# A third buffer for the A and D blocks of the first MLP product, and their loads moved up

## The chip, the cores and the metric

The kernel runs on one core of one Trainium2 chip. The metric is the device time of one execution in microseconds (us). The engines are named as the profile names them: PE is TensorE (PEld its weight loads), DVE is VectorE, ACT is ScalarE, POOL is GpSimd and SP is SyncE. SP and POOL do no arithmetic here that matters; they issue transfers.

## What is computed

One decoder layer over 512 positions of width 1024 in float32: RMSNorm, an input projection whose columns feed a gated linear recurrence (HGRN2) and a block-sparse attention (MoBA), an output projection, cross-attention into 256 memory tokens, and an MLP with a squared ReLU, each with its residual. The change lies in the MLP:

```python
h = rms_norm(x, norm_mlp[l])
x = x + jnp.square(jax.nn.relu(h @ w_ff1[l])) @ w_ff2[l]
return rms_norm(x, norm_final)
```

`w_ff1` is 1024 x 4096 and `w_ff2` is 4096 x 1024.

## The kernel before

**Split weights.** Each 128 x 1024 unit of weights is loaded in float32 into a raw buffer (`wr`, or `wA`, `wB`, `wC`, `wc`, `wD`, `wd` in the first MLP product) and split into a high part that ACT writes (`wh`) and a low part that DVE writes (`wl = raw - wh`). Each product is then three matmuls: high by high, high by low, low by high.

**The first MLP product** (`f1_group`, line 1107) runs in eight groups j. In each, a 2 x 2 block product is made with seven products instead of eight, the way of Strassen and Winograd, on sums and differences of blocks. A group is seven steps of 24 matmuls. Of the weights it needs seven operands, in this order of splitting: A, B, D, C, A, c, D. `f1_load` (277) loads a block by a transfer on SP; for B and c a second transfer on POOL adds another block into the buffer when the first has landed (`accum_op`, 283). The second A is the sum B + C and the second D is D + A; DVE makes both in place, in the buffers of A and D (`f1_add`, 285). So the buffers of A and D are read until late in a group: that of A until the split of the fifth operand, that of D until that of the seventh.

**Buffers.** `raw_tile` (227) gives them out in turn: B, C and c have the three buffers of tag `raw`, A and D the two of tag `rawl` in the pool `late`, which takes the place of the pool `early` once that is closed (1034). A load waits until the last reader of its buffer is done.

**The order** around the change is written out by hand. `need` (315) runs at the start of step s of the program with u the unit that TensorE takes next, and prepares the unit two ahead (`SPLIT_AHEAD`): `f1_prep` (288) issues its split and, by s, loads for the next group. Instructions of one engine run in the order of the program, and SP's and POOL's transfers are issued in the order of their queues. DVE's queue holds, beside the low parts and the sums, the additions that take the finished products out of TensorE's banks (`evac`); `t <- t, X` is one of them. `more_sums` (222) issues further transfers that nothing in this product reads: sums of blocks of `w_ff2`, written to the tensors `u` (copies on SP, adds on POOL).

**The second MLP product** takes its units in order through `load_unit` (232), from both tags of buffers, two of five from `rawl`.

Of the kernel before, what the change touches and what calls it, by code (L numbers as in the profile page):

```python
# [8 lines left out]
F32 = mybir.dt.float32  # L9
# [6 lines left out]
P = 128  # L16
D = 1024
T = 512
M = 256
# [12 lines left out]
MLP = 8 + 8 + 4 + 8 + 4 + 4 + 4 + 4 + 8 + 8 + 8  # L32
FF2 = MLP + 7 * 8
# [89 lines left out]
def hybrid_layer(ctx: ExitStack, tc: tile.TileContext, xT, memT, ws, vecs, consts, rots, out):  # L123
    nc = tc.nc
    pace = Pace()
    V, A, PE = (pace.engine(e, t) for e, t in ((nc.vector, "dve"), (nc.scalar, "act"), (nc.tensor, "pe")))
    SY, PO = pace.engine(nc.sync, "dma"), pace.engine(nc.gpsimd, "pool")
    cpool = ctx.enter_context(tc.tile_pool(name="cpool", bufs=1))
# [4 lines left out]
    ep = early.enter_context(tc.tile_pool(name="early", bufs=1, reuse_waits="tile"))  # L133
# [36 lines left out]
    raws, his, los, late, n8 = {}, {}, {}, [], [1]  # L170
    state = {"load": 0, "split": 0}
    LOAD_AHEAD, SPLIT_AHEAD, RAWS = 6, 2, 3
# [13 lines left out]
    def two(ap):  # L186
        return ap.rearrange("p (n c) -> p n c", n=2)
# [34 lines left out]
    def more_sums():  # L222
        dma = next(transfers, None)
        if dma is not None:
            tc.add_manual_dep(dma.ins, marks[-2].ins.name, AFTER)

    def raw_tile(name, in_late):
        if in_late:
            return late[0].tile([P, D], F32, tag="rawl", name=name, bufs=2)
        return wpool.tile([P, D], F32, tag="raw", name=name, bufs=RAWS)  # L230

    def load_unit(parts=((0, D),)):
        u = state["load"]
        raws[u] = raw_tile(f"wr{u}", u >= FF2 and (u - FF2) % 5 in (1, 3))
        for a, b in parts:
            SY.dma_start(raws[u][:, a:b], sources[u][:, a:b])
        state["load"] += 1
        if SUMS_FROM <= u < MLP:
            more_sums()
# [6 lines left out]
    def split_raw(u, raw, a, b, eng=None):  # L246
        A.activation(his[u][:, a:b], raw[:, a:b], AF.Copy)

        def lower(hi=his[u], lo=los[u]):
            (eng or V).tensor_sub(lo[:, a:b], raw[:, a:b], hi[:, a:b].bitcast(F32))  # L250
        later(lower)
# [4 lines left out]
    def split_begin():  # L256
        u = state["split"]
        his[u] = wpool.tile([P, D], F32R, tag="whi", name=f"wh{u}", bufs=WBUFS)
        if u < MLP - 4 and u % 4 == 0:
            los[u] = ep.tile([P, D], F32R, tag="wloe", name=f"wl{u}", bufs=1)  # L260
        else:
            los[u] = wpool.tile([P, D], F32R, tag="wlo", name=f"wl{u}", bufs=WBUFS - 1)
        state["split"] += 1
        return u

    def split_unit(eng=None):
        u = split_begin()
        split_part(u, 0, D, eng)
        del raws[u]
# [7 lines left out]
    def f1_load(j, what):  # L277

        r, c = {"A": (0, 0), "B": (0, 0), "C": (1, 1), "D": (1, 0)}[what.upper()]
        t = f1raw[what, j] = raw_tile(f"w{what}{j}", what in "AD")  # L280
        nc.sync.dma_start(two(t), E[r][c][j].rearrange("n p c -> p n c"))
        if what in "Bc":
            nc.gpsimd.dma_start(two(t), E[0][1][j].rearrange("n p c -> p n c"), accum_op=ALU.add)

    def f1_add(j, out, x, y):
        V.tensor_add(f1raw[out, j], f1raw[x, j], f1raw[y, j])

    def f1_prep(j, s):

        split_raw(split_begin(), f1raw[("ABCAcDd" if j == 7 else "ABDCAcD")[s], j], 0, D)  # L290
        if s == 1:
            f1_add(j, "A", "B", "C")
        if j == 7:
            if s == 1:
                f1_load(j, "d")
                state["load"] = FF2
            elif s > 2:
                load_unit()
            if s == 3:
                f1_add(j, "d", "d", "A")  # L300
        elif s == 1:
            f1_load(j + 1, "B")
        elif s == 3:
            f1_add(j, "D", "D", "A")
            f1_load(j + 1, "C")
        elif s == 4:
            f1_load(j + 1, "A")
        elif s == 5:
            f1_load(j + 1, "c")
        elif s == 6:  # L310
            f1_load(j + 1, "D")
        if s in (2, 6):
            more_sums()

    def need(u):
        marks.append(last_mm[0])
        if MLP <= u + SPLIT_AHEAD < FF2:
            f1_prep(*divmod(u + SPLIT_AHEAD - MLP, 7))
            return
        last = MLP if u < MLP else UNITS  # L320
        most = RAWS if u < MLP else RAWS + 2
        want_load, want_split = min(last, u + LOAD_AHEAD + 1), min(last, u + SPLIT_AHEAD + 1)
        while state["split"] < want_split or state["load"] < want_load:
            if state["load"] < want_load and state["load"] - state["split"] < most:
                load_unit()
            elif state["split"] < want_split:
                split_unit()
            else:
                break
        if MLP - 6 <= u < MLP - 2:  # L330
            for what in ("A", "B", "CD", "c")[u - MLP + 6]:
                f1_load(0, what)
# [68 lines left out]
    def fm_stage(u0, act, n, evac, name, groups, order=tuple(range(KT)), o=slice(None)):  # L401


        u = 0
        for size, late in groups:
            accs = []
            early, rest = order[:KT - late], order[KT - late:]
            for j in range(size):
                need(u0 + u + j)
                accs.append(acc_bank(f"{name}{u + j}"))  # L410
                for k in early:
                    fm_k(u0 + u + j, accs[j][:, :n], act, k, k == order[0], k == order[-1], o)
                if not late:
                    evac(u + j, accs[j])
            if late:
                for j in range(size):
                    for k in rest:
                        fm_k(u0 + u + j, accs[j][:, :n], act, k, False, k == order[-1], o)
                    evac(u + j, accs[j])
            u += size  # L420

    def tm_stage(u0, act, ntok, evac, name):

        accs = [acc_bank(f"{name}{t}") for t in range(ntok)]
        for j in range(4):
            need(u0 + j)
            hi, lo = his[u0 + j], los[u0 + j]
            for t in range(ntok):
                for kk in range(2):
                    a_hi, a_lo = act(2 * j + kk)  # L430
                    a_hi, a_lo = a_hi[:, t * P:(t + 1) * P], a_lo[:, t * P:(t + 1) * P]
                    w_hi, w_lo = hi[:, kk * T:(kk + 1) * T], lo[:, kk * T:(kk + 1) * T]
                    st = j == 0 and kk == 0
                    mm(accs[t], a_hi, w_hi, st, False)
                    mm(accs[t], a_hi, w_lo, False, False)
                    mm(accs[t], a_lo, w_hi, False, j == 3 and kk == 1)
                if j == 3:
                    evac(t, accs[t])
# [24 lines left out]
    A.dma_start(vec, vecs)  # L463
    load_x(0)
    load_unit(((0, 2 * P),))
    load_unit(((0, D // 2),))
    load_x(1)
# [138 lines left out]
    lower_bounds()  # L606
    ordered.__exit__(None, None, None)
    need(3)
    for k in range(KT):
        fm_k(3, accs[3], x_act, k, k == 0, k == KT - 1)  # L610
# [3 lines left out]
    u = 4  # L614
# [242 lines left out]
        yield from norm_rows(S, M, rbm, rcm)  # L857

    mem = {}
    rbm = cpool.tile([P, M], F32, name="rbm")  # L860
    rcm = cpool.tile([P, 2], F32, name="rcm")
    fm_stage(u, x_act, T, ev_g, "hg", ONE * 4)
    u += 4
# [523 lines left out]
```

## Time and profile before

| | |
|---|---|
| three timed runs | 758.73, 760.6, 762.17 us; median 760.6 us |
| the profiled execution | 756.95 us, of which its span from first to last instruction is 755.2 us |
| granted TensorE clock, mean | 0.996 of full |
| busy share of the span | PE 97%, PEld 88%, DVE 72%, ACT 55%, POOL 7% |
| transfers | 137.03 MB, mean 181 GB/s |

The rows below come from the profiled execution. A busy share is an average over stages with different limits, so the stage of the change is read by itself, from the load of one group's B to that of the next. An engine that is idle and not waited for costs nothing. Matmuls are pipelined; a row of one lasts about 0.28 us, and the next starts 0.12 us behind it.

### The profile page before, as it was taken

What the parts mean: (1) busy time and instruction counts of PE and PEld (TensorE: products, weight loads), DVE (VectorE), ACT (ScalarE), POOL (GpSimd) and SP (SyncE); (2) the same over time, 40 slices, a digit from 0 to 9 for tenths busy, and PEclk for the clock granted to TensorE, in tenths of its full rate; (3) what the DMA queues carried; (4) which work ended last, traced back from release to release, by engine and by line L of the source; (5) the groups of instructions that cost most, each with busy time, mean ns of one, the idle gap of its engine ahead of it and who ended that gap; (6) DMA issues with size and microseconds to landing.
All of it is one profiled execution on the core that took longest, in us unless ns stands there. A gap on an engine that the chain in (4) does not pass through costs nothing.

```text
span 755.2 us, 11996 instructions
## 1 busy us (share of the span) xinstructions
PE 735.1 (97%) x4696; PEld 664.0 (88%) x4696; DVE 545.5 (72%) x891; ACT 415.5 (55%) x634; POOL 49.4 (7%) x62
## 2 busy tenths in 40 slices
PE   7999999999999999999999999998999999999995
PEld 5888888777787998888888999998899999999995
DVE  6898554887766656767377878786778778877783
ACT  6773447345855454545365655465446655546562
POOL 1000000000111200011000111221110000000000
PEclk9999999999999999999999999999999999999999
DMA  7425334544689996479726688898975655545641
GB/s 274 149 76 167 112 116 135 167 135 132 183 207 238 207 313 258 118 160 278 254 77 147 169 249 221 187 208 215 212 213 169 204 189 193 173 162 168 207 156 57
DMA packets 44441, 137.03 MB, mean 181 GB/s; under 512 B 4544, under 2 KB 6976, under 8 KB 43744
## 3 DMA queue, kind: packets, MB, share of 16 engines
q1 hardware_dynamic: 34944, 110.64, 42.8%
q0 software_dynamic: 8960, 25.17, 19.1%
q8 instruction: 37, 0.61, 0.3%
q10 hardware_dynamic: 480, 0.45, 0.2%
q14 instruction: 20, 0.16, 0.1%
HBM read 134.15 MB, written 35.65 MB: 225 GB/s over the span
## 4 chain that ended last, share of the span: by engine, by line
PE 87%; DMA 4%; ACT 3%; DVE 3%; issue 2%; SPq 0%; DVEq 0%; ACTq 0%
PE X L115 19%; PE Y L115 12%; PE xo L115 7%; PE mkq L115 6%; PE xq L115 6%; PE wo L115 5%; DMA wA<-in_ws_dram 3%; PE hf L115 3%; PE Z L115 3%; PE hg L115 3%; PE mv L115 3%; PE memv L115 3%; PE hq L115 3%; PE hi L115 3%; PE memk L115 2%
## 5 line engine op out<-in xcount | busy, mean ns | idle before, releaser
L115 ACT ACTIVATE wh<-wr 128x1024 fp32r<-128x1024 f32 (+2 forms) x126 | 130.4, 1041 | 121.2 <-PE wo L115 19.6
L115 DVE TENSOR_TENSOR wl<-wr,wh 128x1024 fp32r<-128x1024 f32 (+2 forms) x126 | 151.5, 1205 | 40.7 <-ACT wh L115 26.4
L115 PE MATMUL X<-op,wh 128*128 128x256 f32 x512 | 92.7, 283 | 0.0
L115 PEld LDWEIGHTS X<-op,wh 128*128 128x128 f32 x512 | 79.9, 192 | 0.1
L115 PE MATMUL X<-op,wl 128*128 128x256 f32 x256 | 72.7, 284 | 0.6 <-DVE wl L115 0.6
L200 POOL DMA_DIRECT2D u<-in_ws_dram x32 | 31.0, 968 | 328.5 <-PE hg L115 201.1
L115 PEld LDWEIGHTS X<-op,wl 128*128 128x128 f32 x256 | 49.1, 192 | 0.8 <-DVE wl L115 0.8
L115 PE MATMUL Y<-OS,wh 128*128 128x256 f32 x256 | 47.2, 284 | 0.2 <-ACT t L115 0.2
L115 PE MATMUL X<-OS,wh 128*128 128x256 f32 x256 | 46.5, 283 | 0.0
L115 PE MATMUL Y<-op,wh 128*128 128x256 f32 x256 | 46.2, 283 | 0.0
L115 PEld LDWEIGHTS Y<-OS,wh 128*128 128x128 f32 x256 | 39.9, 192 | 0.5 <-ACT t L115 0.4
L115 PEld LDWEIGHTS Y<-op,wh 128*128 128x128 f32 x256 | 39.9, 192 | 0.0
L115 PEld LDWEIGHTS X<-OS,wh 128*128 128x128 f32 x256 | 39.9, 192 | 0.0
L115 PE MATMUL Y<-op,wl 128*128 128x256 f32 x128 | 36.2, 283 | 0.0
L115 PE MATMUL X<-OS,wl 128*128 128x256 f32 x128 | 36.2, 283 | 0.0
L115 PE MATMUL Y<-OS,wl 128*128 128x256 f32 x128 | 36.2, 283 | 0.0
L115 ACT ACTIVATE g<-t 128x512 f32<-128x512 f32 x32 | 19.0, 624 | 29.2 <-DVE t L115 29.2
L115 ACT ACTIVATE op<-g 128x1024 fp32r<-128x1024 f32 x28 | 29.2, 1045 | 0.5 <-PE X L115 0.5
L115 DVE TENSOR_TENSOR op<-g,op 128x1024 fp32r<-128x1024 f32 x24 | 29.3, 1219 | 0.0
L115 ACT ACT_TABLE_LOAD x22 | 28.2, 1283 | 1.5 <-PEq L1375 1.2
L115 PE MATMUL mkq<-xhi,wh 128*128 128x512 f32 x64 | 26.7, 417 | 0.0
L115 ACT ACTIVATE t<-X 128x256 f32<-128x256 f32 x32 | 11.3, 375 | 27.8 <-PE X L115 27.7
(312 smaller groups left out, 2114.2 us busy)
## 6 DMA issues: line engine op xcount, KB each, us to landing
wr<-in_ws_dram SPq DMA_DIRECT2D x90, 512.0 KB, 4.3
u<-in_ws_dram POOLq DMA_DIRECT2D x32, 512.0 KB, 7.7
wr<-u SPq DMA_DIRECT2D x32, 512.0 KB, 3.4
u<-in_ws_dram SPq DMA_DIRECT2D x16, 512.0 KB, 3.9
u<-u SPq DMA_DIRECT2D x16, 512.0 KB, 4.7
wA<-in_ws_dram SPq DMA_DIRECT2D x8, 512.0 KB, 6.5
wD<-in_ws_dram SPq DMA_DIRECT2D x8, 512.0 KB, 6.3
wB<-in_ws_dram SPq DMA_DIRECT2D x8, 512.0 KB, 4.3
```

What stands on the lines that cost most here:

```text
L115: return f(*args, **kw)
L200: return nc.gpsimd.dma_start(dst, src, accum_op=ALU.add, max_dma_last_dim=4 * D)
```

## The change

The tag `rawl` gets three buffers instead of two (`RAWS` is 3). The load of the next group's A is issued in the part of `f1_prep` for s = 2 instead of s = 4, that is behind the load of B and ahead of a transfer of `more_sums` and the load of C. In the second MLP product every second unit is taken from `rawl` instead of two of five, and the limit of loads ahead of the splits is 6 instead of 5. For the memory of the third buffer `rbm`, a tile of 128 x 256 that the memory's keys are scaled with, moves from a pool that stays open to the pool `early`.

```diff
--- before.py
+++ after.py
@@ -226,12 +226,12 @@
 
     def raw_tile(name, in_late):
         if in_late:
-            return late[0].tile([P, D], F32, tag="rawl", name=name, bufs=2)
+            return late[0].tile([P, D], F32, tag="rawl", name=name, bufs=RAWS)
         return wpool.tile([P, D], F32, tag="raw", name=name, bufs=RAWS)
 
     def load_unit(parts=((0, D),)):
         u = state["load"]
-        raws[u] = raw_tile(f"wr{u}", u >= FF2 and (u - FF2) % 5 in (1, 3))
+        raws[u] = raw_tile(f"wr{u}", u >= FF2 and (u - FF2) % 2 == 1)
         for a, b in parts:
             SY.dma_start(raws[u][:, a:b], sources[u][:, a:b])
         state["load"] += 1
@@ -300,11 +300,11 @@
                 f1_add(j, "d", "d", "A")
         elif s == 1:
             f1_load(j + 1, "B")
+        elif s == 2:
+            f1_load(j + 1, "A")
         elif s == 3:
             f1_add(j, "D", "D", "A")
             f1_load(j + 1, "C")
-        elif s == 4:
-            f1_load(j + 1, "A")
         elif s == 5:
             f1_load(j + 1, "c")
         elif s == 6:
@@ -318,7 +318,7 @@
             f1_prep(*divmod(u + SPLIT_AHEAD - MLP, 7))
             return
         last = MLP if u < MLP else UNITS
-        most = RAWS if u < MLP else RAWS + 2
+        most = RAWS if u < MLP else 2 * RAWS
         want_load, want_split = min(last, u + LOAD_AHEAD + 1), min(last, u + SPLIT_AHEAD + 1)
         while state["split"] < want_split or state["load"] < want_load:
             if state["load"] < want_load and state["load"] - state["split"] < most:
@@ -857,7 +857,7 @@
         yield from norm_rows(S, M, rbm, rcm)
 
     mem = {}
-    rbm = cpool.tile([P, M], F32, name="rbm")
+    rbm = ep.tile([P, M], F32, name="rbm")
     rcm = cpool.tile([P, 2], F32, name="rcm")
     fm_stage(u, x_act, T, ev_g, "hg", ONE * 4)
     u += 4
```

What this does to SP's queue, in the middle of the first MLP product. The names are those of the blocks with the group's number behind the letter; in brackets are the semaphores that the issue waits for (DMAHW and DMASW are landings of earlier transfers, DVE, Activation and PE the engines). Before, the loads for group 3:

```order
L281 DMA wB3_4307<-in_ws_dram 128x2x512 [waits DMASW4_49,DMAHW2_49,DVE_49,Activation_49]
L281 DMA wC3_4383<-in_ws_dram 128x2x512 [waits DMAHW5_49,DMAHW3_49,DVE_49]
L281 DMA wA3_4419<-in_ws_dram 128x2x512 [waits DMAHW6_49,DMAHW4_49,DVE_49]
L281 DMA wc3_4455<-in_ws_dram 128x2x512 [waits DMASW5_49,DVE_49]
L281 DMA wD3_4486<-in_ws_dram 128x2x512 [waits DMAHW0_49,DVE_49]
```

and now:

```order
L281 DMA wB3_4307<-in_ws_dram 128x2x512 [waits DMASW4_49,DMAHW2_49,DVE_49,Activation_49]
L281 DMA wA3_4346<-in_ws_dram 128x2x512 [waits DMAHW3_49]
L281 DMA wC3_4385<-in_ws_dram 128x2x512 [waits DMAHW6_49,DMAHW4_49,DVE_49]
L281 DMA wc3_4455<-in_ws_dram 128x2x512 [waits DMAHW5_49,DMASW5_49,DVE_49]
L281 DMA wD3_4486<-in_ws_dram 128x2x512
```

The load of A stands directly behind that of B, one load and, in one group, a copy of `u` earlier, and it has lost its wait for DVE, as has the load of D.

At the start of the MLP, ahead of the first groups' loads (`wr66` and `wr67` are the last units of the stage before). Before:

```order
L115 DMA wr66_3458<-in_ws_dram 128x1024 [waits DMAHW6_49,DVE_49]
L281 DMA wA0_3570<-in_ws_dram 128x2x512
L281 DMA wD0_3661<-in_ws_dram 128x2x512 [waits DMAHW7_49]
L115 DMA wr67_3567<-in_ws_dram 128x1024 [waits DMAHW0_49,DVE_49,Activation_49]
L281 DMA wB0_3609<-in_ws_dram 128x2x512 [waits DMAHW1_49,DMAHW2_49,DVE_49,Activation_49]
```

and now:

```order
L115 DMA wr66_3458<-in_ws_dram 128x1024 [waits DMAHW6_49,DVE_49]
L281 DMA wA0_3570<-in_ws_dram 128x2x512
L281 DMA wD0_3661<-in_ws_dram 128x2x512 [waits DMAHW7_49]
L281 DMA wA1_3850<-in_ws_dram 128x2x512 [waits DMAHW0_49]
L115 DMA wr67_3567<-in_ws_dram 128x1024 [waits DMAHW1_49,DVE_49,Activation_49]
L281 DMA wB0_3609<-in_ws_dram 128x2x512 [waits DMAHW2_49,DVE_49,Activation_49]
```

The load of A for group 1 has moved up to here, where its new buffer is free; it stood behind the load of C for group 1. PE's, DVE's, ACT's and POOL's instructions keep their order.

## Rows read from the trace of the kernel before

**Rows 1.** The page: the span; busy time of TensorE (us, share of the span, instructions); the chain that ended last, by line.

```profile
span 755.2 us, 11996 instructions
...
PE 735.1 (97%) x4696; PEld 664.0 (88%) x4696; DVE 545.5 (72%) x891; ACT 415.5 (55%) x634; POOL 49.4 (7%) x62
...
PE X L115 19%; PE Y L115 12%; PE xo L115 7%; PE mkq L115 6%; PE xq L115 6%; PE wo L115 5%; DMA wA<-in_ws_dram 3%; PE hf L115 3%; PE Z L115 3%; PE hg L115 3%; PE mv L115 3%; PE memv L115 3%; PE hq L115 3%; PE hi L115 3%; PE memk L115 2%
```

**Rows 2.** The stretch view of the first MLP product, one row for each of five groups, cut where SP issues the load of the next B. Columns: the stretch and its length, then busy time and (instructions) of PE, PEld, DVE, ACT and POOL, the granted clock of TensorE, the busy share of the DMA engines, GB/s.

```profile
455.01:475.18 20.17, 20.17 (x170) 20.17 (x169) 16.62 (x23) 11.11 (x17) 4.23 (x4) 1.00 0.77 200
475.18:496.40 21.22, 21.05 (x176) 20.84 (x175) 15.55 (x22) 11.10 (x17) 2.74 (x3) 1.00 0.88 221
496.40:519.56 23.16, 20.41 (x171) 20.21 (x170) 16.60 (x23) 12.27 (x18) 5.78 (x6) 1.00 0.89 211
519.56:541.80 22.24, 20.42 (x165) 20.21 (x164) 15.47 (x22) 10.98 (x17) 4.26 (x4) 0.96 0.86 211
541.80:562.81 21.01, 21.01 (x170) 21.01 (x170) 16.70 (x23) 11.21 (x17) 2.47 (x2) 0.96 0.84 205
```

**Rows 3.** The waits of two stretches: the first two rows from 413 to 600 us (the first MLP product), the last from 575 to 755 us (the second). Engine and tile, who it waited for: us in total, times, longest.

```profile
PEld X L115 <- DVE t L115: 5.4, 3, 3.0
...
ACT wh L115 <- DMA wA<-in_ws_dram: 8.5, 4, 3.9
...
PE X L115 <- DVE wl L115: 0.6, 1, 0.6
```

**Rows 4.** The chain of waits from 455 to 585 us, in order of time: start, duration, what.

```profile
484.00 7.33 DMA wA<-in_ws_dram
...
504.07 1.13 DVE wl L115
...
505.24 9.27 DMA wA<-in_ws_dram
...
514.58 1.06 ACT wh L115
```

**Rows 5.** The timeline of DVE (VectorE) around the end of the group from 455 us (first three rows) and of that from 496 us: start, duration, engine, line, operation, output <- inputs, and in brackets the idle time before it with what ended it.

```profile
471.28 1.22 DVE L115 TENSOR_TENSOR wl<-wA,wh 128x1024 fp32r<-128x1024 f32 x1
472.42 0.42 DVE L115 TENSOR_TENSOR t<-t,X 128x256 f32<-128x256 f32 x1
...
477.95 1.23 DVE L115 TENSOR_TENSOR wl<-wD,wh 128x1024 fp32r<-128x1024 f32 x1 [0.98 <-ACT wh L115]
...
515.67 1.23 DVE L115 TENSOR_TENSOR wl<-wA,wh 128x1024 fp32r<-128x1024 f32 x1 [3.56 <-ACT wh L115]
516.82 0.41 DVE L115 TENSOR_TENSOR t<-t,X 128x256 f32<-128x256 f32 x1
```

**Rows 6.** The timeline of PE (TensorE matmuls): the first matmul behind each of its two longest pauses in this stage.

```profile
517.28 0.39 PE L115 MATMUL X<-OBh,wh 128*128 128x256 f32 x1 [2.75 <-DVE t L115]
...
539.52 0.39 PE L115 MATMUL X<-OBh,wh 128*128 128x256 f32 x1 [1.82 <-DVE t L115]
```

**Rows 7.** The stretch view again, of one microsecond in the first of these pauses and of four behind the second; columns as in group 2.

```profile
516.00:517.00 1.00, 0.00 (x0) 0.00 (x0) 1.00 (x2) 0.59 (x1) 0.58 (x1) 1.00 0.05 16
...
540.00:544.00 4.00, 4.00 (x24) 4.00 (x23) 3.61 (x6) 1.63 (x3) 1.26 (x2) 0.57 0.71 123
```

**Rows 8.** The timeline of SP's queue: the issue of a load of A and of the load of B behind it.

```profile
463.84 0.37 SPq L281 DMA_DIRECT2D wA<-in_ws_dram  x1
...
475.18 0.37 SPq L281 DMA_DIRECT2D wB<-in_ws_dram  x1
```

**Rows 9.** The DMA issues of five short stretches, each of which holds the issue named: A at 463.84 us, B at 455.01 us, B at 475.18 us, the add into B at 482.80 us, the add into B at 527.02 us. The last number is the time from issue to landing, us.

```profile
wA<-in_ws_dram SPq DMA_DIRECT2D x1, 512.0 KB, 6.0
...
wB<-in_ws_dram SPq DMA_DIRECT2D x1, 512.0 KB, 3.2
...
wB<-in_ws_dram SPq DMA_DIRECT2D x1, 512.0 KB, 7.1
...
wB<-in_ws_dram POOLq DMA_DIRECT2D x1, 512.0 KB, 6.8
...
wB<-in_ws_dram POOLq DMA_DIRECT2D x1, 512.0 KB, 7.6
```

**Rows 10.** The timeline of ACT (ScalarE) at the end of the group from 455 us: the splits of the next A and B.

```profile
469.94 1.06 ACT L115 ACTIVATE wh<-wA 128x1024 fp32r<-128x1024 f32 x1
470.91 1.05 ACT L115 ACTIVATE wh<-wB 128x1024 fp32r<-128x1024 f32 x1
```

**Rows 11.** The timeline of SP's queue ahead of the MLP: two issues that follow one another.

```profile
369.23 0.45 SPq L281 DMA_DIRECT2D wD<-in_ws_dram  x1
383.30 0.34 SPq L115 DMA_DIRECT2D wr<-in_ws_dram  x1
```

**Rows 12.** The page's DMA queues: packets, MB, and the time their packets took as a share of the time of 16 engines.

```profile
q1 hardware_dynamic: 34944, 110.64, 42.8%
q0 software_dynamic: 8960, 25.17, 19.1%
```

**Rows 13.** The timeline of POOL's queue: the issues of the adds into B in the groups from 475 and from 519 us.

```profile
482.80 1.23 POOL L283 DMA_DIRECT2D wB<-in_ws_dram  x1 [8.28 <-ACT wh L115]
...
527.02 1.23 POOL L283 DMA_DIRECT2D wB<-in_ws_dram  x1 [8.47 <-DMA wB<-in_ws_dram]
```

## Prediction

> **What bounds the kernel now.** I read the page first, then the stretch view cut into groups of the first MLP product, then the waits, the chain and the timelines of that stage. TensorE is busy for 735.1 us of a span of 755.2 us, and the chain that ended last is TensorE work but for one transfer that stands out: the loads of wA, 3% of the span [rows 1]. Nothing that leaves TensorE's work alone can give more than the 20 us in which it is idle, so the question is what happens around wA.
>
> The stretch view, cut from one load of B to the next, shows where [rows 2]. Seven products of 2.88 us make a group of 20.16 us, and the group from 455.01 takes just that. The next four take 21.22, 23.16, 22.24 and 21.01 us: 87.63 us where four times 20.16 is 80.64, so **6.99 us are lost in four groups**. The waits name the path of it [rows 3]: TensorE's weight loads sit 5.4 us behind DVE's write of t in three places, and ACT sits 8.5 us behind the landing of wA in four. The chain links the two [rows 4]: DVE ends the lower half of the second use of A (504.07 + 1.13 = 505.2), only then the load of the next A is issued (505.24), it takes 9.27 us, and ACT splits A the moment it has landed (514.58). DVE is an in-order queue. In an undisturbed group the lower half of A starts at 471.28 and the addition into t right behind it at 472.42; in the late group they start at 515.67 and 516.82, after 3.56 us of nothing [rows 5]. TensorE's last product accumulates in the bank that this addition reads, so it stops for 2.75 us, and for 1.82 us one group later [rows 6].
>
> Idle of 5.4 us leaves 1.6 of the 6.99 us open. They are in the clock: from 540 to 544 us the granted clock is 0.57 of full with TensorE busy throughout [rows 7], that is mostly the 1.2 GHz level, right behind the 1.82 us pause. 0.43 x 4 = 1.7 us of TensorE's work is lost there, and 5.4 + 1.7 = 7.1 us agrees with 6.99 us. The Trainium skill (TensorE: Matmul & The Clock Gate, HAM oscillation) says that pauses for a DMA between runs of matmuls put the clock back to 1.2 GHz, at a cost of half of the time so clocked; by it a removed pause brings its echo back too (7.0 us), without it only 5.4 us. The trace agrees for the second pause, and shows no fall behind the longer first one.
>
> **The change, part by part.** *The third late buffer and the load of A moved up.* Today A and D share two late buffers, so A of the next group takes the buffer of this group's A, which is read until the fifth of seven products. The load of 463.84 [rows 8] lands 6.0 us later [rows 9], just in time for the split at 469.94 [rows 10]; that of 484.00 again has 6 us and needs 7.33 [rows 4]. With three buffers in the order A, D, A, D, A of the next group takes that of the D of the group before, free since that group's last split. In the changed order its load stands right behind that of B, with no wait for DVE. B of that group is issued at 475.18 [rows 8]; A would follow at some 475.6, 8.4 us sooner. Behind B, which landed 7.1 us after its issue [rows 9], and with 1.53 us of its own (below) it would be there at 483.8; with the 9.27 us of the slowest row of the chain, at 484.9. Its split is due at 490.1 (469.94 and 20.16). It is in time by 5 us or more. Both ends: if A is never late, all 6.99 us come back; if a pause stays that is just too short to matter but still drops the clock, 5.4 us at most. I take 6.99 us, since the undisturbed group shows what a group without the pause takes.
>
> *What A is moved past.* On SP it passes the load of C, which is split only after A, B and D of the next group, and, where there is one, a copy of u, of which no reader comes before the second MLP product; either starts later by A's issue, 0.4 us. POOL's queue is not changed. D, whose load waited for the lower half of D, now waits for that of A two products earlier; it can only come sooner. The first A that has the new buffer moves up before the MLP stage, right behind the load of D at 369.23 [rows 11], into a stretch in which SP then waits 13.6 us (until 383.30): nothing.
>
> *The second MLP product.* Late buffers take every second block there, and six instead of five are in turn; a load may begin one block sooner. TensorE waits there for one lower half, 0.6 us in all [rows 3], and no load stands in that part of the chain: 0 us. *rbm in the early pool*: the same instructions at another address, 0 us.
>
> The sum is -7.0 us against the profiled execution's 756.95 us (span 755.2 and 1.75 around it), that is 749.9 us. The three timed runs have a median of 760.6 us, 3.65 us above it; I take the difference from there: **760.6 - 7.0 = 753.6 us**. If those 3.65 us are more of the same pauses, they go as well and 749.9 us is the lower end.
>
> **The rivals.** *The DMA engines are the bound.* By the page, 48 adds on the software queue took 19.1% of the span, 3.0 us each, and 211 plain transfers (110.64 MB by 0.524 MB) 42.8%, 1.53 us each [rows 12]. A group with five loads, two adds of its own and two adds of u needs 5 x 1.53 + 4 x 3.0 = 19.7 us of 20.16 us: it fits with 0.5 us. The stretch view is worse: 0.89 x 23.16 = 20.6 us [rows 2]. With that, three groups take 61.8 us where they now take 66.62 us: 4.8 us come back, **755.8 us**. For it speaks that an earlier load makes no bandwidth; against it that the engines stand idle while SP and POOL wait (share 0.05 in the stretch from 516 [rows 7]), gaps which A's load would fill. The Trainium skill (DMA: Bandwidth & Descriptors, Issuing engines are not separate DMA queues) says that transfers of all issuers run on the same 16 engines and interleave, so moving A up only takes the time from another; by that rule this rival's 755.8 us is the time, and the trace bears it out only as far as the share stays near 0.9 in those groups.
>
> *B takes A's place.* B's load is followed by an add on POOL that waits for its landing. B landed 3.2 us after its issue in the group of 455.01, but 7.1 us in that of 475.18, where two adds were in flight; its add was issued at 482.80 and took 6.8 us [rows 9, 13], so B was ready at 489.6, its split due at 491.07 (470.91 [rows 10] plus 20.16): 1.5 us to spare. In the group of 519.56, 527.02 plus 7.6 is 534.6 against 535.46 (15.9 us behind B's issue, as 470.91 is behind 455.01): 0.85 us. Behind that, DVE is idle for 0.98 us before the next lower half [rows 5]. So B may come about 1.8 us later before TensorE feels it, and A in the same queue costs it at most A's own 1.53 us. It holds, barely; A gone from the time of B's add helps. If B is 4 us later instead, each of three groups loses 4.0 - 1.8 = 2.2 us, 6.6 us, and the time is **760.2 us**: no change.
>
> *Contention on the other side.* More transfers in flight at once may cost more each, C and c then come late too. With 13% on the 19.7 us a group takes the 22.2 us that the three late ones take on average now; that is the point from which it decides. At 25% (24.6 us) three groups lose 2.4 us each: **767.8 us**. For it: with two adds in flight B took 7.1 us instead of 3.2 us. Against it: that is waiting in line, not more work, as the bytes per second of the late groups, 211 to 221, are not below the 200 of the punctual one [rows 2].
>
> *The change does not do what it says*: A's load stands behind B's in SP's queue, and B's waits for DVE. But that is the wait of today's B, met at 475.18 us, and the load of A has none for DVE of its own. I count it with the second rival.
>
> **How the numbers follow.** Forecast 0.63 (753.6 us), DMA bound 0.13 (755.8 us), B in A's place 0.16 (760.2 us), contention 0.08 (767.8 us). A measurement of this kernel tells about 0.5%, 3.8 us, from no change, so faster means under 756.8 us. The forecast and three quarters of the first rival lie there: 0.73. The rest of it and the second rival are 0.19, contention 0.08. The range goes from 749.9 us (all of the 3.65 us too) to 759.0 us, which takes in the first rival and B late by up to 3.6 us (three times 1.8 us behind the forecast); outside lie contention, the second rival's upper half, and little below.
>
> **What would show it.** Right: cut from load of B to load of B, every group takes 20.2 us; no DMA of wA in the chain; TensorE's wait for DVE's t under 0.5 us; the clock 1.00 from 540 to 544 less what the shift moves; A issued 0.4 us behind B and landed by 10 us. Wrong: ACT waits for wB or wc instead, POOL's add of B is issued over 9 us behind B's load, or groups of 20.6 us with a share over 0.95. If the late groups go and the time still stays above 757 us, my carrying of the profiled 7.0 us to the timed runs is what failed.

## The result, and the profile after

The changed kernel takes 750.05 us (median of 6 runs, 749.68 to 750.2); the kernel before, in 6 runs of which three are new, 758.68 us (757.2 to 762.17). The ratio of the runs is 0.9879, 95% interval 0.9857 to 0.9902, so 8.6 us are gone. The profiled executions are 756.95 and 750.14 us, 6.8 us apart. I had forecast 753.6 us and a difference of 7.0 us: the difference of the two profiled executions was right, the one of the timed runs was too small.

The page of the changed kernel: the span, TensorE, the chain by line.

```profile
span 748.3 us, 11983 instructions
...
PE 731.8 (98%) x4696; PEld 660.9 (88%) x4696; DVE 545.2 (73%) x891; ACT 415.1 (55%) x634; POOL 49.5 (7%) x62
...
PE X L115 24%; PE Y L115 15%; PE xo L115 7%; PE mkq L115 6%; PE xq L115 6%; PE wo L115 5%; PE Z L115 3%; PE hg L115 3%; PE mv L115 3%; PE memv L115 3%; PE hq L115 3%; PE hi L115 3%; PE memk L115 2%; PE hf L115 2%; PE xs L115 2%; PE a L115 1%
```

No transfer is left among the costly lines of the chain, against [rows 1]. The stretch view, cut again from load of B to load of B, columns as in [rows 2]:

```profile
455.12:475.28 20.16, 20.16 (x170) 20.16 (x169) 16.60 (x23) 10.98 (x17) 4.24 (x4) 1.00 0.80 199
475.28:495.43 20.15, 20.15 (x170) 20.15 (x169) 15.46 (x22) 10.99 (x17) 3.13 (x4) 1.00 0.91 228
495.43:515.59 20.16, 20.16 (x170) 20.16 (x169) 16.60 (x23) 12.27 (x18) 4.17 (x6) 1.00 0.95 236
515.59:535.75 20.16, 20.16 (x170) 20.16 (x169) 15.46 (x22) 10.99 (x17) 4.07 (x5) 1.00 0.94 236
535.75:555.91 20.16, 20.16 (x170) 20.16 (x169) 16.61 (x23) 10.99 (x17) 3.90 (x4) 1.00 0.87 216
```

Every group takes 20.16 us at full clock, where the four from 475 us took 21.0 to 23.2. The share of the DMA engines goes up to 0.95, above the 0.89 of the groups before, with nothing lost. What is left of the waits of [rows 3] from 405 to 590 us:

```profile
ACT wh L115 <- DMA wc<-in_ws_dram: 0.5, 1, 0.5
...
PE Y L115 <- ACT t L115: 0.2, 1, 0.2
```

TensorE waits for nothing that DVE writes. SP's queue, the landings of B (issued at 475.28) and A (475.70) and of A at 516.05, and ACT's splits of that first A and B; they answer to [rows 8, 9, 10]:

```profile
475.28 0.37 SPq L281 DMA_DIRECT2D wB<-in_ws_dram  x1
475.70 0.52 SPq L281 DMA_DIRECT2D wA<-in_ws_dram  x1
```

```profile
wB<-in_ws_dram SPq DMA_DIRECT2D x1, 512.0 KB, 7.3
...
wA<-in_ws_dram SPq DMA_DIRECT2D x1, 512.0 KB, 8.2
...
wA<-in_ws_dram SPq DMA_DIRECT2D x1, 512.0 KB, 10.8
```

```profile
490.05 1.05 ACT L115 ACTIVATE wh<-wA 128x1024 fp32r<-128x1024 f32 x1
491.00 1.05 ACT L115 ACTIVATE wh<-wB 128x1024 fp32r<-128x1024 f32 x1
```

A goes out 0.42 us behind B. It lands at 483.9 (475.70 + 8.2), where I had worked out 483.8, and is split at 490.05, when ACT comes to it. The longest landing, 10.8 us, is more than any of A in the rows of before (9.3 us) and than the 10 us I had set as a sign, and still 3.5 us early (516.05 + 10.8 = 526.9, split at 530.4).

### The profile page after: what moved, and what is told of

The parts are those of the page before. It is cut to its first block, busy times and chain, and to the rows that moved or that the text cites. A ratio compares the mean times of both kernels' runs of the same rounds, so it can differ in the third digit from the quotient of the medians.

```text
span 748.3 us, 11983 instructions
## 1 busy us (share of the span) xinstructions
PE 731.8 (98%) x4696; PEld 660.9 (88%) x4696; DVE 545.2 (73%) x891; ACT 415.1 (55%) x634; POOL 49.5 (7%) x62
## 4 chain that ended last, share of the span: by engine, by line
PE 94%; DVE 2%; ACT 1%; DMA 1%; issue 1%; DVEq 0%; ACTq 0%
PE X L115 24%; PE Y L115 15%; PE xo L115 7%; PE mkq L115 6%; PE xq L115 6%; PE wo L115 5%; PE Z L115 3%; PE hg L115 3%; PE mv L115 3%; PE memv L115 3%; PE hq L115 3%; PE hi L115 3%; PE memk L115 2%; PE hf L115 2%; PE xs L115 2%; PE a L115 1%
## 5 line engine op out<-in xcount | busy, mean ns | idle before, releaser
L115 ACT ACTIVATE t<-X 128x256 f32<-128x256 f32 x32 | 11.3, 377 | 28.0 <-PE X L115 27.9
```

The source lines that it names most:

```text
L115: return f(*args, **kw)
```

## The experiments

Ratios are to the kernel before, run on the same chip in turn.

**Is it one stage, and is its loss always 7.0 us?** The kernel before, unchanged, timed again and profiled three more times.

> The kernel before, unchanged, for the clock and span of each run. Theory 1 (the late loads of A vary from run to run, and the first profiled execution had few of them): its runs spread over 3 to 5 us, the longer ones at a lower mean clock, and a new profile whose groups of the first MLP product lose another sum than 7.0 us, about as much more as its time is above 757 us. Rival (what the timed runs have above the profile lies elsewhere): the groups lose 7.0 +- 0.5 us again whatever the time, and the difference is in another stage. Ratio 1.00 for both.

> The kernel before, once more, for another profile. Theory (the spread of its runs lies in the six groups of the first MLP product alone): what lies ahead of the load of B at 435 us and behind the load of d at 563 us takes 434.9 and 192.4 us within 0.3 us, as in the profiles so far, and the span less 627.3 us is the time of the six groups, 120.96 us and the pauses. Rival: one of the other two parts is longer where the time is longer.

> The same kernel and the same expectations as the run ahead of it; a third new profile for the spread of the pauses.

Measured: 758.76 us (757.42 to 760.81, 12 runs; ratio 1.0005, 0.9990 to 1.0020); the other two executions 759.39 and 760.61 us. Cut at SP's issues of the load of B at 435 us and of d at 563 us, the profiles give (us):

| profile | ahead of the groups | six groups | lost of 120.96 | behind | span |
|---|---|---|---|---|---|
| before, the first | 434.85 | 127.96 | 7.0 | 192.39 | 755.2 |
| before, timed again | 435.07 | 128.22 | 7.3 | 192.31 | 755.6 |
| before, second look | 435.07 | 130.17 | 9.2 | 192.36 | 757.6 |
| before, third look | 434.89 | 131.59 | 10.6 | 192.32 | 758.8 |
| changed | 434.95 | 120.96 | 0.0 | 192.39 | 748.3 |

The first theory holds, without a rest: both outer parts stay within 0.25 us, and all the spread is in the six groups. What differs in the longest execution, first by its stretches, then by the two falls of the clock (columns as in [rows 2]), then by its waits:

```profile
455.56:477.63 22.07, 20.54 (x172) 20.34 (x171) 16.60 (x23) 10.98 (x17) 4.23 (x4) 1.00 0.76 196
...
497.14:521.39 24.25, 21.06 (x167) 20.86 (x166) 16.61 (x23) 12.38 (x18) 6.40 (x6) 0.95 0.88 215
...
521.39:545.48 24.09, 21.93 (x169) 21.73 (x169) 15.66 (x22) 11.20 (x17) 4.26 (x4) 0.93 0.83 196
```

```profile
518.00:526.00 8.00, 6.89 (x44) 6.89 (x45) 6.42 (x9) 4.45 (x9) 2.13 (x2) 0.79 0.79 144
542.00:550.00 8.00, 6.80 (x44) 6.80 (x45) 7.02 (x10) 4.45 (x9) 2.13 (x2) 0.79 0.78 144
```

```profile
ACT wh L115 <- DMA wA<-in_ws_dram: 11.6, 5, 4.4
...
PEld X L115 <- DVE t L115: 7.5, 3, 3.4
```

There a pause of TensorE comes in the second group already, and the clock falls behind both of the later pauses: to a mean of 0.79 of full over 8 us, which is 0.21 x 8 = 1.7 us each. The pauses of 7.5 us and 3.4 us in the clock are 10.9 us, against 10.6 us lost. In the first profile one of its two long pauses had no such fall. So 7.0 us was the least of four, and a timed run loses 8.3 us: 758.4 us (its median beside the other experiments), less 1.8 us around the span and 627.3 us outside the groups, is 129.3 us, where six undisturbed groups take 120.96 us.

**The buffer without the earlier place.** The changed kernel with the load of A back at its old place:

```diff
-        elif s == 2:
-            f1_load(j + 1, "A")
...
+        elif s == 4:
+            f1_load(j + 1, "A")
```

> The changed kernel, but the load of A is issued at its old place in the program (s = 4, behind the load of C). Theory 1 (what counts is how long the load has before its split): A no longer waits for DVE, so it goes out right behind C, 6.6 us behind B instead of 8.8 us, 2.2 us sooner; A was late by 1.3, 3.9 and some 3 us in three groups, so two small pauses are left, 5 to 6 of the 8.6 us come back (753 to 754 us, ratio 0.992 to 0.994). Rival (the place in the queue does it, the buffer only makes it possible): ratio 0.998 to 1.00.

Measured: 755.17 us (752.65 to 758.46), ratio 0.9955 (0.9937 to 0.9972): 3.4 us back, less than the 5 to 6 expected, and the spread is as wide as before. In the profile (an execution of 757.32 us) the load of A is free of DVE, but still behind C and in the middle of the adds; two stretches and the one load of A in the chain:

```profile
495.21:521.11 25.90, 21.06 (x167) 20.86 (x166) 16.70 (x23) 12.38 (x18) 6.40 (x6) 0.93 0.81 192
521.11:543.02 21.91, 21.91 (x173) 21.91 (x172) 15.56 (x22) 11.20 (x17) 4.26 (x4) 0.93 0.85 212
```

```profile
502.20 13.85 DMA wA<-in_ws_dram
516.13 1.06 ACT wh L115
```

A takes 13.85 us to land, longer than any A in the four profiles of before (4.4 to 11.3 us). It went out 1.9 us earlier than before (7.0 us behind B, where [rows 8, 9] have 8.8), not the 2.2 us that I expected, and that is not enough where landings vary by more.

**The earlier place without the buffer.** The kernel before, with `f1_load(j + 1, "A")` moved as in the change, two late buffers.

> The kernel before with the load of A moved behind the load of B in SP's queue, but still two late buffers. Theory 1: SP holds at A's load until DVE has ended the lower half of the second use of A, as before 8.8 us behind B, and C and what stands behind it wait with it. A then has no C ahead of it in the queue, 1.4 us: between 0 and 3 us come back (ratio 0.996 to 1.00). Rival (the earlier place alone is worth it): ratio 0.988. A worse rival: C and c come too late, ratio over 1.005.

Measured: 756.66 us, ratio 0.9973 (0.9959 to 0.9987): 2 us back, as expected. SP holds at A's load, and what stands behind it goes out later. Loads in the chain of that profile:

```profile
484.53 10.32 DMA wB<-in_ws_dram
...
507.29 9.23 DMA wA<-in_ws_dram
```

A is late as before, and now B's add (the first of the two) too. The two halves bring 3.4 and 2.0 us by themselves and over 8 us together: the buffer takes away the wait for DVE, the earlier place the transfers ahead of A.

**The adds of u out of the way.** The kernel before with two late buffers, and all sums of blocks of w_ff2 issued ahead of the MLP.

```diff
         if SUMS_FROM <= u < MLP:
             more_sums()
+            if u % 4 == 0:
+                more_sums()
```

> The kernel before, with the copies and adds of u all issued ahead of the MLP (one more at every fourth unit), so that the groups have five loads and two adds each and none of u. Theory 1 (A's 6 us are short only where adds of u are in flight): no pause, every group 20.16 us, and the same 7 to 9 us come back with two buffers (750 to 752 us, ratio 0.988 to 0.991) unless the denser transfers cost something ahead. Rival (6 us are too short in any case): at least 4 us of pauses are left in the groups, ratio above 0.994.

Measured: 751.45 us (751.27 to 751.74), ratio 0.9903 (0.9886 to 0.9920). Two of its groups:

```profile
476.98:497.14 20.16, 20.16 (x170) 20.16 (x169) 15.47 (x22) 10.98 (x17) 2.42 (x2) 1.00 0.65 172
497.14:517.30 20.16, 20.16 (x170) 20.16 (x169) 16.61 (x23) 12.26 (x18) 2.41 (x2) 1.00 0.71 186
```

All six take 20.16 us, so A's old 6 us are enough when no transfers of u are in flight: its six landings take 3.8 to 4.9 us here. The edit moves copies and adds of u together and does not tell the two apart. The load of B at 435 us comes at 436.67 here: 1.8 us are paid ahead, where at 204 us ACT now waits 1.6 us for a load (`mraw`, the memory tokens), which it does not in the kernel before or the changed one. That is where the 1.4 us go by which it trails the changed kernel.

**How near the DMA engines are to their limit.** The changed kernel, with copies of 512 KB to a spare tensor added.

```diff
+        if j < 7 and s in (4,):
+            nc.sync.dma_start(spare[2 * j + (s > 3)], ws[MLP + 16 * (j // 2) + s])
```

In the second run the steps are (0, 4), in the last (6,): there the copy stands behind the loads of c and D.

> The changed kernel with one more copy of 512 KB in each of seven groups, from a weight to a spare tensor in DRAM that nothing reads, issued on SP for s = 4, so behind the load of C. By the page's prices (1.53 us a transfer, 3.0 us an add) a group with two adds of u then needs 21.2 us of the DMA engines where it has 20.16: were they the true price, four groups would lose about 1 us each, 754 us, ratio to the kernel before 0.994. If the prices hold time in line as well as work (the groups now have a share of 0.95 and no pause), the copy goes into the gaps: 750 to 751 us, ratio 0.988 to 0.990, with the landings of A and c later and pauses of at most 0.5 us.

> As the run ahead of it, with two such copies a group (for s = 0 and s = 4). By the page's prices 22.8 us a group: four groups lose 2.6 us each and their echo in the clock, 760 us or more, ratio about 1.00. If a third of the price is waiting in line: some 19.5 us of work, between 750 and 755 us, with the first pauses behind B or c rather than A.

> The changed kernel with one more copy of 512 KB a group, as the run with the copy behind the load of C, but issued for s = 6, behind the load of D and, in some groups, ahead of the load of B. If the DMA engines' work bounds the groups once 1.5 us are added to 19.7, the place does not matter: 755 us again, ratio 0.995 to 0.997. If it was the place (the copy stood ahead of c, whose add on POOL waits for its landing), it costs at most 1.5 us here: 750 to 752 us, ratio 0.988 to 0.991, and only a pause behind B.

Measured: 755.61 us (ratio 0.9958, 0.9943 to 0.9974), 756.0 us (0.9967, 0.9951 to 0.9983) and **750.06 us** (0.9892, 0.9872 to 0.9911). The first alone looked like the limit of the engines, as the page's prices have it. The second did not fit that (0.4 us more, where by the prices it had to be 760 us or over), and the third ends it: the same copy two loads later costs nothing. Waits of the first and then of the last (both 405 to 600 us), and two groups of the last:

```profile
ACT wh L115 <- DMA wB<-in_ws_dram: 9.0, 3, 4.3
...
ACT wh L115 <- DMA wc<-in_ws_dram: 5.7, 3, 2.9
...
PE Y L115 <- ACT t L115: 3.5, 2, 3.3
```

```profile
ACT wh L115 <- DMA wc<-in_ws_dram: 4.6, 2, 2.7
...
ACT wh L115 <- DMA wB<-in_ws_dram: 0.5, 1, 0.5
...
PE Y L115 <- ACT t L115: 0.2, 1, 0.2
```

```profile
495.49:515.65 20.16, 20.16 (x171) 20.16 (x170) 16.59 (x23) 12.38 (x18) 2.99 (x3) 1.00 1.00 259
515.65:535.81 20.16, 20.16 (x171) 20.16 (x170) 15.46 (x22) 11.10 (x17) 4.26 (x4) 1.00 1.01 253
```

ACT waits for c about as long in both, and the last loses nothing by it; what the first has more is the wait for B. Its longest, and the pause of TensorE that follows in the same stretch:

```profile
556.56 1.06 ACT L115 ACTIVATE wh<-wB 128x1024 fp32r<-128x1024 f32 x1 [4.33 <-DMA wB<-in_ws_dram]
```

```profile
565.68 0.70 PE L115 MATMUL Y<-OS,wh 128*128 128x256 f32 x2 [3.30 <-ACT t L115]
```

ACT's queue has no wait for a transfer between these two, so t comes late because B's split did, and the pause and the fall of the clock behind it (1.7 us) are most of the 5.6 us by which the run is longer than the changed kernel. B is late by its add on POOL: in the three last groups the add lands 13.1, 13.4 and 14.4 us after its issue, with the copy issued 2.4 to 3.0 us behind it; with the copy behind D 9.6, 11.8 and 10.5 us, with no copy 6.9, 7.5 and 9.4 us. The engines have a share of 1.00 in the last run's groups of 20.16 us. So what decides is what is in flight beside a transfer that has a time to keep, not the sum of the work. That the copy slows the add by taking turns with it is argued from these landings; no run isolates it.

**The second MLP product.** The changed kernel with `(u - FF2) % 5 in (1, 3)` and `RAWS + 2` put back.

> The changed kernel with the two edits of the second MLP product undone (two of five units from the late buffers, five loads ahead); the third late buffer stays. Theory: they are worth nothing, 749.7 to 750.3 us, ratio to the kernel before 0.987 to 0.991, and the part behind the load of d takes 192.4 us. Rival (a load that may begin one block sooner saves the 0.6 us that TensorE waits there): 750.6 us or more, that part 193 us.

Measured: 750.02 us (749.74 to 750.36), ratio 0.9891 (0.9872 to 0.9911), the part behind the groups 192.3 us. These two edits are worth nothing, as the sum had them.

No experiment points to a version that beats the changed kernel: its groups are TensorE's 20.16 us at full clock, and the other edits tried cost or changed nothing.

## Why the prediction was right or wrong

**The mechanism** was right. A's load was held by DVE's second lower half, landed late where transfers of u were in flight, and stopped TensorE through ACT's and DVE's queues. Each half alone and the run without transfers of u in the groups show it, and the groups take what the undisturbed one took.

**The step that failed** is the carrying to the timed runs: "I take the difference from there: 760.6 - 7.0 = 753.6 us". Both numbers were off. 7.0 us was the loss of one execution, the least of four that are now profiled (7.0 to 10.6), where the timed runs lost 8.6 us (8.3 us beside the other experiments); and 760.6 us was the median of three runs, where all six have 758.68 us and later ones 758.3 to 758.8 us. Of the 3.55 us between forecast and measurement 1.9 are this base and 1.6 the loss. The text had the right hint (the 3.65 us between profile and median "are more of the same pauses"), but as an end of the range, so that 750.05 us lies on its edge. As the outer parts of the span do not vary, the forecast could have been made without any difference: 627.3 us, six groups of 20.16 us and 1.8 us are 750.1 us. The sum against the profile's own time, 749.9 us, was that number.

**The clock.** The 1.7 us for the fall came back, and in two of four executions it is paid twice. In the four profiles of before TensorE pauses eight times for over 1 us, and the clock fell behind six of them: one of two in the first profile, the only one in the second, both in the third and two of three in the fourth. The length of the pause does not tell which: there was no fall behind 1.53 and 2.75 us, but one behind each of 1.81, 1.82 and 2.16 us. The Trainium skill (TensorE: Matmul & The Clock Gate, HAM oscillation) has a wait for a DMA put the clock back each time, in an example whose waits are longer than most of these; the trace agrees for the six and not for the two.

**What A is moved past, the second product, rbm**: nothing, as said; D's load was issued 12.0 us behind B's (487.25), where it had been 12.9 us (488.10).

**DMA bound** (0.13): did not come. The price of 19.7 us a group is more than the work: with one copy more the page's prices give 21.2 us, and the groups still took 20.16. The Trainium skill (DMA: Bandwidth & Descriptors, Issuing engines are not separate DMA queues) says that transfers interleave on the same engines whoever issues them. The trace agrees: A, issued among more transfers, takes up to 10.8 us where the first profile had up to 9.3 us; it has the time now. Of the sign I had named for this rival, groups of 20.6 us with a share over 0.95, the share alone is no sign: 1.00 went with no loss.

**B in A's place** (0.16): did not come. B landed 7.3 us after its issue in the group where I had 7.1 with 1.53 to bear, and its add, 7.5 us from 523.12 us, ended 0.7 us ahead of its split at 531.32 in a later one. That the limit is near the two runs with copies behind the load of C show: there B is late, by 9.0 and 12.8 us of ACT's waiting. ACT's wait for c, which I had named beside that for B, is no sign of a loss: the run with the second product as before has 5.0 us of it in 750.02 us. **Contention** (0.08): no.

## What to carry to other kernels

When executions of a kernel spread by more than the gain, find the part of the span that spreads and count from what it takes undisturbed; one profile's loss is one draw. Here a load that must keep a time needed both its buffer and its place in the queue early, and what a further transfer cost depended on what was in flight beside it. A busy share near 1.00 of the DMA engines said nothing of lateness by itself: it went with no loss in one run and with 5.6 us in another.

## What was not expected of the hardware

The landings of one 512 KB load, that of A, take 4.4 to 11.3 us over the groups and executions of the kernel before, and 4.4 to 13.9 us in one execution with the third buffer only; with the transfers of u out of the groups 3.8 to 4.9 us. Where TensorE comes to wait for them, that made a spread of 5 to 7 us in 758; without such waits six runs lie within 0.5 us. Sixteen DMA engines carried six plain loads or copies and four adds of 512 KB in 20.16 us, at a share of 1.00, with TensorE at full clock throughout.
